# Strassen products in both feed-forward networks of a two-layer trunk, with the activations through DRAM

## The chip, the core and the metric

The kernel runs on one core of a Trainium2 chip. The metric is the device time of one execution in microseconds (us). In the text PE is the matmul engine (TensorE), PEld its weight load, DVE VectorE, ACT ScalarE, POOL GpSimd, and SP the queue that issues most DMAs.

## What is computed

Two layers over 1024 tokens of width 1024, in fp32. Layer 0 is an mLSTM (chunkwise recurrence with a gate on its output), layer 1 attention with forget gates ("fox" in the code). Behind each stands a feed-forward network (FFN), which holds the two products of this case. Norms stand before and after each block, with a residual.

```python
D_MODEL = 1024
SEQ = 1024
D_FF = 2816
CONV_WIDTH = 3
...
def conv_ffn(h, w_up, conv_w, conv_b, w_down):
    S = h.shape[1]
    u = h @ w_up
    up = jnp.pad(u, ((0, 0), (CONV_WIDTH - 1, 0), (0, 0)))
    y = conv_b
    for j in range(CONV_WIDTH):
        y = y + conv_w[j] * up[:, j:j + S]
    gate, val = jnp.split(y, 2, axis=-1)
    return (jax.nn.gelu(gate, approximate=True) * val) @ w_down
...
    # mlstm_mixer, behind the recurrence
    hs = hs.reshape(B, S, H * DV) * w_head_norm.astype(f32)
    hs = hs * jax.nn.sigmoid(o.astype(f32))
    return hs.astype(h.dtype) @ w_out
```

## The kernel before

Every fp32 operand is split in two float32r parts, hi (a cast on ACT, `split`, L155) and lo (source minus hi, on DVE, L156), and every product is three matmuls: hi by hi, hi by lo, lo by hi. The token side stands transposed in SBUF as `xh` and `xl` [128, 8, 1024]. Other SBUF space is numbered slots of [128, 1024]. PSUM is one tile of two banks, `two`, and six banks `b0` to `b5`, of 512 columns.

The FFN (`ffn`) goes through 22 column tiles f of 128. For each, gate and value are 2 x 2 x 24 matmuls of 128x512 (L689, two halves of tokens, 8 row tiles, 3 terms). The convolution reads PSUM (ACT L698, two taps on DVE L702), then gelu (L748) and the product with the value (L749); the result is split and kept in SBUF. Every two column tiles `down` adds their products for each of the 8 token tiles (L722, 1056 matmuls per layer) to accumulators `yacc` in SBUF (DVE L728). Weights are loaded one tile ahead (`load_w`, `load_rows`). The last four column tiles are added token tile by token tile; each is finished by `tail_a` (norm, residual, store) and, in the first FFN, `tail_b` (the next norm); `tail_a` multiplies on DVE (L172) and divides the residual add between POOL (L174, 416 columns) and DVE (L175). Residuals are loaded to three slots in turn, L765.

The recurrence goes through 8 chunks of 128 tokens. The output gate of all chunks is projected in four groups of 256 columns (`o_tile`, L345 tanh), stored to DRAM (`m_so`) and loaded again per chunk (`gate`). Groups 0 and 1 come before the recurrence, 2 and 3 partly among chunk 0 and 1. The output projection of chunk i-1 (`project`, L266) fills PE while DVE and ACT do chunk i. At the end 84 matmuls of the FFN's first column tile stand between the projection of chunk 7 and the transposes of its tokens (`turn_next`, by `tail_c`, L164). The attention's output projection has the same arrangement. Two helpers appear in the rows only: L242 (`acc`) is the matmuls of the mLSTM's and attention's projections and of the last token tile, and L1084 and L786 are products of two SBUF tiles on POOL, of 1024 columns in the attention and of 512 in the last tail.

The order on PE is that of the code (within `in_order`); the other engines' order is set by a scheduler from the program. The stages in the trace: projections of the mLSTM to 266.8 us, recurrence to 503.6, first FFN to about 1256, attention to about 1957, second FFN to the end.

Of the kernel before, what the change touches and what calls it, by code (L numbers as in the profile page):

```python
# [35 lines left out]
# the slots of more than 1024 columns  # L36
WIDE = {14: 1032, 31: 1032, 0: 1088, 1: 1088, 2: 1088, 3: 1088, 15: 1088, 27: 1088, 29: 1088, 30: 1088}


class Core:  # L40
    """Shared state: constants, the transposed activations in two float32r parts, the SBUF slots that every
    phase lays out for itself ([128, 1024] each), and the PSUM as one tile of two banks and six of one."""

    def __init__(self, ctx, tc):
# [14 lines left out]
        self.xh = c.tile([P, ND, S], F32R, name="xh")  # L59
        self.xl = c.tile([P, ND, S], F32R, name="xl")  # L60
# [4 lines left out]
        self.nring = 0  # L65
        self.slots = {}
# [15 lines left out]

    def wide(self, *banks):
# [12 lines left out]
    def in_order(self):  # L96
        """Within this the tensor engine takes its instructions in the order given here."""
# [31 lines left out]
    def rms_scale(self, src, root=True):  # L129
        """1 / sqrt(mean(src^2) + eps) over the free axis of a [128, 1024] view; root: from the table's root."""  # L130
# [22 lines left out]
    def split(self, hi, lo, src):  # L153
        """src in two float32r parts."""
# [3 lines left out]
    def transpose_split(self, h, hi, lo, banks):  # L158
        """h [128 rows, 8*128] -> its 8 transposed blocks, split, in hi / lo [128, 8, 128]."""
        for b in range(2):  # L160
            tp = self.b[banks[b]].rearrange("p (d t) -> p d t", d=4)
            for d in range(4):
                e = 4 * b + d
                self.nc.tensor.transpose(tp[:, d], h[:, e * P:(e + 1) * P], self.ident)  # L164
            self.split(hi[:, 4 * b:4 * b + 4], lo[:, 4 * b:4 * b + 4], tp)
# [12 lines left out]
    def tail_b(self, h, z, g, root=True):  # L178
        """h = z / rms(z), times g."""
# [1172 lines left out]
```

## Time and profile before

| | us |
|---|---|
| median of 3 runs (2700.39 to 2707.19) | 2703.64 |
| span of the profiled execution | 2699.6 |
| PE busy | 2632.5 (98%) |
| DVE busy | 1379.2 (51%) |
| ACT busy | 920.5 (34%) |
| POOL busy | 289.1 (11%) |
| weight loads (PEld) busy | 2192.3 (81%) |
| mean granted clock of PE | 0.992 |

The busy times are sums over the whole span; a stage is read from the windows of the section on rows. The profiled span leaves out what lies around the first and the last instruction.

### The profile page before, as it was taken

Reading aid. Unit: us, or ns where it says so; the run is one execution under the profiler, and the core shown is the slowest. Engines: PE = TensorE matmul, PEld = TensorE weight load, DVE = VectorE, ACT = ScalarE, POOL = GpSimd, SP = SyncE. Lnnn points to the kernel's source line nnn. Section 1 sums busy time; section 2 is a strip of 40 time slices with the busy share of each in tenths; the row PEclk is TensorE's granted clock in tenths of the full one; section 3 lists DMA queues with packets and bytes.
Section 4 is the critical chain, followed back from the end, with each engine's and each line's share of the span. In section 5 each row is a group of like instructions: output and inputs, shape, how many; then the busy total and the mean of one; then the engine's idle time right before and its main releaser. Section 6 shows DMA issues by size and latency. Waiting matters only on the chain.

```text
span 2699.6 us, 33977 instructions
## 1 busy us (share of the span) xinstructions
PE 2632.5 (98%) x13344; PEld 2192.3 (81%) x13344; DVE 1379.2 (51%) x2404; ACT 920.5 (34%) x1697; POOL 289.1 (11%) x321
## 2 busy tenths in 40 slices
PE   8999888999999999999999999999999999999998
PEld 7989877888888888888878888877888888888886
DVE  5222266644444444448565565556643455555546
ACT  5222233332222222225355455555333222222222
POOL 0001111000000000003133333322100000000001
PEclk9999899999999999999999999999999999999999
DMA  7444353311111111123755444545311111111123
GB/s 209 141 140 137 105 161 114 110 32 47 48 50 51 49 50 51 48 71 137 212 145 153 137 140 134 146 144 164 110 55 47 47 47 47 47 47 47 47 62 118
DMA packets 247133, 259.67 MB, mean 96 GB/s; under 512 B 16701, under 2 KB 208029, under 8 KB 246973
## 3 DMA queue, kind: packets, MB, share of 16 engines
q1 hardware_dynamic: 246828, 257.24, 31.9%
q8 instruction: 105, 1.72, 0.3%
q14 instruction: 56, 0.45, 0.1%
q10 hardware_dynamic: 144, 0.26, 0.0%
HBM read 193.85 MB, written 63.60 MB: 95 GB/s over the span
## 4 chain that ended last, share of the span: by engine, by line
PE 49%; DVE 3%; ACT 1%; DMA 1%; issue 1%; POOL 1%; DVEq 0%; SPq 0%; POOLq 0%; ACTq 0%
PE b L689 18%; PE b L889 9%; PE two L722 4%; PE b L722 4%; PE b L1069 2%; PE b L1057 2%; PE b L266 2%; PE two L1042 2%; PE b L906 2%; PE two L266 1%; PE b L242 1%; PE b L1042 1%; ACT junk L137 1%; DVE s L156 1%; DVE s L172 1%
## 5 line engine op out<-in xcount | busy, mean ns | idle before, releaser
L689 PE MATMUL b<-xh,s 128*128 128x512 f32 (+1 forms) x2816 | 865.5, 388 | 0.7 <-DVE xl L156 0.7
L689 PEld LDWEIGHTS b<-xh,s 128*128 128x128 f32 x2816 | 524.4, 188 | 117.8 <-DVE xl L156 0.9
L156 DVE TENSOR_TENSOR s<-s,s 128x1024 fp32r<-128x1024 f32 (+2 forms) x319 | 314.8, 997 | 496.9 <-ACT s L155 478.1
L689 PE MATMUL b<-xl,s 128*128 128x512 f32 (+1 forms) x1408 | 547.1, 389 | 0.0
L155 ACT CAST s<-s 128x1024 fp32r<-128x1024 f32 (+2 forms) x319 | 264.0, 839 | 663.0 <-PE b L722 226.2
L702 DVE SCALAR_TENSOR_TENSOR s<-b,cp,s 128x512 f32<-128x512 f32 x344 | 241.7, 745 | 232.6 <-ACT s L698 229.6
L689 PEld LDWEIGHTS b<-xl,s 128*128 128x128 f32 x1408 | 264.4, 188 | 58.3
L889 PE MATMUL b<-xh,s 128*128 128x512 f32 x768 | 274.6, 413 | 1.7 <-DVE s L156 1.1
L722 PE MATMUL two<-s,s 128*128 128x512 f32 x1056 | 258.1, 394 | 0.0
L722 PE MATMUL b<-s,s 128*128 128x512 f32 x1032 | 252.3, 394 | 0.0
L722 PEld LDWEIGHTS two<-s,s 128*128 128x128 f32 x1056 | 198.0, 188 | 46.7 <-DVE s L728 0.7
L722 PEld LDWEIGHTS b<-s,s 128*128 128x128 f32 x1032 | 193.6, 188 | 45.0
L698 ACT ACTIVATE s<-b,cp 128x512 f32<-128x512 f32 x172 | 133.1, 774 | 279.3 <-PE b L689 279.3
L242 PE MATMUL b<-s,xh 128*128 128x256 f32 (+1 forms) x864 | 163.2, 290 | 10.5 <-ACT s L345 6.7
L889 PEld LDWEIGHTS b<-xh,s 128*128 128x128 f32 x768 | 143.8, 191 | 25.4 <-DVE s L156 1.6
L889 PE MATMUL b<-xl,s 128*128 128x512 f32 x384 | 159.4, 415 | 0.0
L156 DVE TENSOR_TENSOR s<-b,s 128x512 fp32r<-128x512 f32 (+3 forms) x208 | 111.4, 564 | 75.6 <-ACT s L155 70.0
L242 PEld LDWEIGHTS b<-s,xh 128*128 128x128 f32 x864 | 137.8, 195 | 12.2 <-ACT s L345 6.9
L174 POOL TENSOR_TENSOR s<-s,s 128x416 f32<-128x416 f32 x31 | 45.9, 1480 | 886.9 <-DVE ring L144 698.7
L1049 POOL TENSOR_SCALAR s<-s,ring 128x256 f32<-128x256 f32 (+7 forms) x128 | 100.6, 789 | 313.5 <-DVE ring L1048 290.6
L242 PE MATMUL b<-s,xl 128*128 128x256 f32 (+1 forms) x432 | 124.9, 289 | 0.6 <-DVE xl L156 0.6
L155 ACT CAST s<-b 128x512 fp32r<-128x512 f32 (+3 forms) x208 | 95.9, 489 | 75.2 <-PE b L1057 61.5
(221 smaller groups left out, 3360.9 us busy)
## 6 DMA issues: line engine op xcount, KB each, us to landing
s<-in_ffn_w_up_dram SPq DMA_DIRECT2D x88, 512.0 KB, 3.8
s<-in_ffn_w_down_dram SPq DMA_DIRECT2D x44, 512.0 KB, 3.6
s<-in_mlstm_w_in_dram SPq DMA_DIRECT2D x24, 512.0 KB, 6.1
x<-s SPq DMA_DIRECT2D x24, 512.0 KB, 2.6
s<-x SPq DMA_DIRECT2D x24, 512.0 KB, 3.8
s<-in_x_dram SPq DMA_DIRECT2D x16, 512.0 KB, 4.6
s<-in_kv_w_dram SPq DMA_DIRECT2D x16, 512.0 KB, 5.0
f_v<-s SPq DMA_DIRECT2D x32, 256.0 KB, 2.6
```

The lines of the kernel that those rows point to most:

```text
L155: self.nc.scalar.copy(hi, src)
L156: self.nc.vector.tensor_tensor(lo, src, hi, ALU.subtract)
L242: self.nc.tensor.matmul(out, st, mv, start=i == 0, stop=i == n - 1)
L266: self.nc.tensor.matmul(self.at(ps, c), st, mv[:, c:c + 512], start=kk == 0 and st is sh and mv is wh, stop=kk == 7 and st is sl)
L689: nc.tensor.matmul(k.at(u, c, n), st[d], mv[:, d, cs], start=d == 0 and i == 0 and c % 512 == 0, stop=d == ND - 1 and i == 2 and c + n in ...
L698: nc.scalar.activation(y[:, a:b], v, AF.Identity, bias=cp[:, 3, col:col + 1], scale=cp[:, 2, col:col + 1])
L702: nc.vector.scalar_tensor_tensor(y[:, a + j:e], v[:, :e - a - j], cp[:, 2 - j, col:col + 1], y[:, a + j:e], ALU.mult, ALU.add)
L722: nc.tensor.matmul(k.at(ps, c), st[:, cs], mv[:, c:c + 512], start=n == 0 and i == 0, stop=n == len(items) - 1 and i == 2)
L889: nc.tensor.matmul(ps, st[d], mv[:, d, cs], start=d == 0 and i == 0, stop=d == ND - 1 and i == 2)
L906: nc.tensor.matmul(ps, st[:, d, cols], mv[d], start=d == 0 and i == 0, stop=d == ND - 1 and i == 2)
L1042: nc.tensor.matmul(ps[:, c:e], st[:, qs], mv[:, c:e], start=a == 0, stop=a == 1 and e < n)
L1049: nc.gpsimd.tensor_scalar(pt[:, :n], pt[:, :n], rd, 1.0, ALU.mult, ALU.mult)
```

## The change

Both FFN products use Strassen's scheme in Winograd's form: each operand is cut in 2 x 2 blocks, and 7 products of blocks take the place of 8, with sums of blocks as operands.

- Up product: per column tile f the 7 products (`PRODUCTS`) have 12 matmuls of 128x512 each (`up`). Sums on the token side are made once per layer, when a token tile of the second half is turned (`turn`: an add on DVE, six on POOL, splits). Sums of weights are four POOL adds of 512 columns per f (`prep_up`), with five splits. Products go from PSUM to SBUF by an ACT copy or a DVE add, and the convolution reads SBUF. The result is stored to DRAM (`act`), not kept.
- Down product: groups of 4, 3, 2 and 2 pairs of column tiles. The operands of a group are loaded from DRAM in quarters (`load_down`), summed on POOL (`sums_down`) and split (`prep_down`); 7 products over 4 token tiles of 3 matmuls for each pair (`down`).
- Output gate: groups 1 to 3 are projected for the next chunk among the parts of the recurrence (`o_more`) and stay in SBUF. The output projection no longer stands in the recurrence: `out_stage` does it behind, for the mLSTM and the attention alike, token tiles in the order 0, 4, 1, 5, 2, 3, 6, 7.
- Slots are numbered anew, some as pairs of 2048 columns, and `x` is one tile of four blocks.

```diff
+PRODUCTS = ("11", "12", "S2", "S1", "S3", "S4", "22")
...
-    def project(c, i=NT, o=None, nxt=None):
...
+        for i in range(NT):
             nxt = loads(i + 1) if i < NT - 1 else None
             nd = numerators(i, cur)
+            o_more(i + 1, 1)
+            update(i, cur, (0, 1))
+            update(i, cur, (2, 3))
             heads(i, *nd)
...
+            o_more(i + 1, 2)
+            if nxt:
+                scores(i + 1, nxt)
...
+            o_more(i + 1, 3)
...
+            turn_heads(i)
...
+        t21 = k.transposed(h, 0, banks[0])
+        nc.scalar.copy(a21, t21)
+        t22 = k.transposed(h, 1, banks[1])
+        nc.vector.tensor_tensor(s1, t22, a21, ALU.add)
...
+        for name, out, terms in (("S2", s2, ((s1, a11[0], ALU.subtract), (s2, a11[1], ALU.subtract))),
+                                 ("S3", a21, ((a11[0], a21, ALU.subtract), (a21, a11[1], ALU.add))),
+                                 ("S4", s4, ((a12[0], s2, ALU.subtract), (s4, a12[1], ALU.add)))):
+            for a, b, op in terms:
+                nc.gpsimd.tensor_tensor(out, a, b, op)
+            k.split(self.place(name, 0, m), self.place(name, 1, m), out)
...
+        elif name == "S2":
+            nc.gpsimd.tensor_tensor(t1, b12, b11, ALU.subtract)
+            nc.gpsimd.tensor_tensor(t2, b22, t1, ALU.subtract)
+            nc.gpsimd.tensor_tensor(b12, b22, b12, ALU.subtract)
+            nc.gpsimd.tensor_tensor(b21, b21, t2, ALU.subtract)
+        elif name == "S1":
+            split("T2", tmp, 1024)
...
+        for d in range(4):
+            for i, (a, b) in enumerate(((0, 0), (0, 1), (1, 0))):
+                mv = x[b](d)
+                out = bank if name in ("11", "12", "22", "S3") else bank.rearrange("p (m t) -> p m t", m=2)
+                nc.tensor.matmul(out, w[a][:, d], mv, start=first and d == 0 and i == 0, stop=d == 3 and i == 2,
+                                 skip_group_check=True)
...
+        if adds:
+            nc.vector.tensor_tensor(out, out, bank, ALU.add)
+        else:
+            nc.scalar.copy(out, bank)
...
+    GROUPS = (0, 4), (4, 3), (7, 2)
+    LAST = 9, 2
...
+        if i == 0:
+            tt("S1", "A21", "A22", add)
+            tt("A21", "A11", "A21", sub)
+            tt("A11", "S1", "A11", sub)
+            tt("B11", "B12", "B11", sub)
+            tt("T2", "B22", "B11", sub)
+            tt("B12", "B22", "B12", sub)
+        elif i == 1:
+            tt("A12", "A12", "A11", sub)
+            tt("B21", "B21", "T2", sub)
...
+        for p in range(n):
+            for e, (st, mv) in enumerate(((ah, bh), (ah, bl), (al, bh))):
+                nc.tensor.matmul(bank, st[:, p, cs], mv[:, p], start=first and p == 0 and e == 0, stop=p == n - 1 and e == 2,
+                                 skip_group_check=True)
...
+            self.load_down(0, ("A11", "B11"))
+            for name in PRODUCTS:
+                self.steps_up(f, (name,))
+                self.load_down(0, {"S2": ("A12", "B21", "A21"), "S1": ("A22", "B12"), "22": ("B22",)}.get(name, ()))
...
+    def res(self, t):
+        r = self.k.f((31, 32)[t // 4])
...
+def out_stage(k, w, gather, src, dst, gpost, gnext, f, begun=0):
...
+        y = y_of(n)
+        k.out_proj(y, t, w, begun if n == 0 else 0, 5)
+        if n > 1:
+            f.turn(z_of(n), ORDER[n - 2], (0, 1))
+        k.out_proj(y, t, w, 5, 8)
...
+    f.turn(z_of(6), ORDER[6], (0, 1))
+    f.start()
+    f.lead()
+    f.lead2()
+    f.turn(z_of(7), ORDER[7], (0, 1))
+    f.run()
```

Three places in the order of the engines, names of buffers with their numbers.

PE at the entry of the first FFN, before: the projection of chunk 7 (L266, banks b4 and b5) with the transposes of chunk 6's tokens (L164) within it.

```order
L266 MATMUL b_89<-s_130,xl 128x512
L266 MATMUL b_90<-s_130,xl 128x512
L164 MATMUL b_85<-ident,s_2933 128x128 x4
L164 MATMUL b_86<-ident,s_2933 128x128 x4
L266 MATMUL b_89<-s_131,xh 128x512
```

The same place after: end of the projection (L296), the transposes of tile 6 (s_2064), four products of column tiles 0 and 1 (L768), the transposes of tile 7 (s_129), and the third product of column tile 0.

```order
L296 MATMUL two<-p_867,x 128x512 x2
L197 MATMUL b_84<-ident,s_2064 128x128 x4
L197 MATMUL b_85<-ident,s_2064 128x128 x4
L768 MATMUL b_86<-x,s_3424 128x512 x12
L768 MATMUL b_87<-x,s_3425 128x512 x12
L768 MATMUL b_88<-x,s_3424 128x512 x12
L768 MATMUL b_89<-x,s_3425 128x512 x12
L197 MATMUL b_84<-ident,s_129 128x128 x4
L197 MATMUL b_85<-ident,s_129 128x128 x4
L768 MATMUL b_86<-p_3790,s_1828 128x512
```

Between the last two turns there were 84 matmuls of the FFN and the rest of chunk 7's projection; now there are 48 matmuls.

POOL at that place, before: the recurrence's last work, then residual adds (L174) and, much later, weights of the attention (L217).

```order
L510 TENSOR_TENSOR s_156<-s_156,decb 128x516
L174 TENSOR_TENSOR s_818<-s_818,s_2933 128x416
L174 TENSOR_TENSOR s_3121<-s_3121,s_2933 128x416
L174 TENSOR_TENSOR s_818<-s_818,s_2933 128x416
L174 TENSOR_TENSOR s_3121<-s_3121,s_2933 128x416
L217 TENSOR_TENSOR s_129<-s_129,gains 128x1088
```

After: token sums of tile 6 (L700), the residual add of tile 7 (L207), the weight sums of two column tiles (L743 to L746), and then the token sums of tile 7.

```order
L700 TENSOR_TENSOR s_3390<-x,s_3390 128x512
L207 TENSOR_TENSOR s_3420<-s_3420,s_129 128x416
L700 TENSOR_TENSOR s_3390<-s_3390,x 128x512
L743 TENSOR_TENSOR s_554<-s_4198,s_4197 128x512
L744 TENSOR_TENSOR s_554<-s_4197,s_554 128x512
L745 TENSOR_TENSOR s_4198<-s_4197,s_4198 128x512
L746 TENSOR_TENSOR s_4198<-s_4198,s_554 128x512
L743 TENSOR_TENSOR s_554<-s_4218,s_4217 128x512
L744 TENSOR_TENSOR s_554<-s_4217,s_554 128x512
L745 TENSOR_TENSOR s_4218<-s_4217,s_4218 128x512
L746 TENSOR_TENSOR s_4218<-s_4218,s_554 128x512
L700 TENSOR_TENSOR s_3390<-s_156,x 128x512
```

POOL had no sums here; now eight weight sums stand between the two tiles' token sums.

SP at the end, before: residual loads (L765) and stores of the result (L176), three slots in turn.

```order
L765 DMA s_2937<-x_93 128x1024
L765 DMA s_13654<-x_93 128x1024
L765 DMA s_13578<-x_93 128x1024
L176 DMA out_dram<-s_2937 128x1024
L765 DMA s_2937<-x_93 128x1024
L176 DMA out_dram<-s_13654 128x1024
```

After: two slots, the loads (L976) behind the stores (L209) of the pair before.

```order
L976 DMA s_156<-x_92 128x1024
L976 DMA s_2064<-x_92 128x1024
L209 DMA out_dram<-s_156 128x1024
L209 DMA out_dram<-s_2064 128x1024
L976 DMA s_156<-x_92 128x1024
L976 DMA s_2064<-x_92 128x1024
```

A load waits for a store of the round before, where one of three slots had been free.

## Rows read from the trace of the kernel before

**Rows 1.** Page, span and busy us of each engine (share of span).

```profile
span 2699.6 us, 33977 instructions
PE 2632.5 (98%) x13344; PEld 2192.3 (81%) x13344; DVE 1379.2 (51%) x2404; ACT 920.5 (34%) x1697; POOL 289.1 (11%) x321
```

**Rows 2.** Windows: stretch, length, busy by engine, granted clock, DMA share, GB/s.

```profile
0.00:12.00 12.00, 1.97 (x9) 1.60 (x9) 4.73 (x13) 5.20 (x7) 2.70 (x21) 1.00 0.86 285
...
266.80:503.60 236.80, 209.71 (x1210) 178.49 (x1208) 129.86 (x458) 76.02 (x250) 27.17 (x33) 0.94 0.44 132
503.60:1256.00 752.40, 751.79 (x3309) 610.42 (x3310) 375.05 (x488) 208.77 (x259) 20.79 (x13) 1.00 0.18 55
```

**Rows 3.** Timeline of PE after waits: start, us, instruction, idle before.

```profile
284.00 0.79 PE L242 MATMUL b<-s,xh 128*128 128x256 f32 x2 [6.73 <-ACT s L345]
...
501.30 0.66 PE L164 MATMUL b<-ident,s 128*128 128x128 f32 x4 [0.79 <-DVE s L562]
...
1266.60 0.49 PE L242 MATMUL b<-s,xh 128*128 128x272 f32 x2 [2.41 <-DVE F L852]
...
1269.56 0.66 PE L242 MATMUL b<-s,xh 128*128 128x272 f32 x2
...
1270.24 0.63 PE L242 MATMUL b<-s,xh 128*128 128x272 f32 x2
...
1270.84 0.42 PE L242 MATMUL b<-s,xh 128*128 128x272 f32 x2
```

**Rows 4.** Windows of steady FFN, PE and PEld: first L689 alone, then L722 twice.

```profile
600.00:1200.00 600.00, 417.43 (x1795) 337.04 (x1796) 1.00 0.17 51
...
600.00:1200.00 600.00, 185.32 (x796) 149.02 (x794) 1.00 0.17 51
2030.00:2600.00 570.00, 196.91 (x846) 158.40 (x844) 1.00 0.17 49
```

**Rows 5.** Timeline of PE, matmuls of 256 columns.

```profile
1965.42 0.40 PE L689 MATMUL b<-xh,s 128*128 128x256 f32 x2
...
1965.77 0.40 PE L689 MATMUL b<-xh,s 128*128 128x256 f32 x2
```

**Rows 6.** Groups by line and form: count, busy us, mean ns, idle before.

```profile
L156 DVE TENSOR_TENSOR s<-s,s 128x1024 fp32r<-128x1024 f32 x211 | 257.6, 1229 | 473.4 <-ACT s L155 461.9 <-DMA s<-m_wi 11.0 <-PE b L1069 0.5
L728 DVE TENSOR_TENSOR s<-s,b 128x512 f32<-128x512 f32 x142 | 91.1, 682 | 42.3 <-PE b L722 42.3
L749 DVE TENSOR_TENSOR s<-s,s 128x1024 f32<-128x1024 f32 x44 | 53.8, 1223 | 2.1 <-ACT s L748 1.2
L155 ACT CAST s<-s 128x1024 fp32r<-128x1024 f32 x211 | 219.1, 1048 | 622.6 <-PE b L722 226.2 <-DMA s<-in_ffn_w_up_dram 170.6 <-DVE s L749 97.2
L748 ACT ACTIVATE s<-s 128x1024 f32<-128x1024 f32 x44 | 46.6, 1060 | 137.2 <-DVE s L702 137.2
L155 ACT CAST xh<-b 128x512 fp32r<-128x512 f32 x80 | 43.5, 586 | 49.9 <-PE b L164 49.6
```

**Rows 7.** Instructions of three lines: count, min/median/max ns, first and last start.

```profile
L172 DVE SCALAR_TENSOR_TENSOR s<-s,ring,s x15: 1274/1285/2369, 1221.5 to 2689.2; 128x1024 f32<-128x1024 f32 x15
L174 POOL TENSOR_TENSOR s<-s,s x31: 1071/1633/1946, 362.0 to 2691.7; 128x416 f32<-128x416 f32 x31
L1084 POOL TENSOR_TENSOR s<-s,s x7: 2382/2393/2398, 1438.9 to 1829.6; 128x1024 f32<-128x1024 f32 x7
```

**Rows 8.** Timeline near the end, all engines: start, us, instruction.

```profile
2684.18 5.74 PE L242 MATMUL b<-s,s 128*128 128x512 f32 x24
2689.17 2.37 DVE L172 SCALAR_TENSOR_TENSOR s<-s,ring,s 128x1024 f32<-128x1024 f32 x1
2689.17 1.28 POOL L786 TENSOR_TENSOR s<-s,s 128x512 f32<-128x512 f32 x1 [2.39 <-DVE ring L146]
```

**Rows 9.** DMA issues: count, KB each, median us from issue to landing.

```profile
x<-s SPq DMA_DIRECT2D x24, 512.0 KB, 2.6
s<-x SPq DMA_DIRECT2D x24, 512.0 KB, 3.8
```

More of the change, by code (lines that the diff above doesn't have):

```diff
@@ L1 @@
 from contextlib import ExitStack
+from copy import copy
 from functools import partial
@@ L81, in r, with both, xb, xs @@
         return self.slot(i, F32R)[:, :n]
+    def both(self, j):
+        self.slot(PAIRS[j][0], F32R)
+        return self.slots[j][0]
+    def xb(self, part, h, kk):
+        o = 4096 * BLOCK[h, kk] + 2048 * part
+        return self.x[:, o:o + 2048].rearrange("p (d t) -> p d t", d=4)
+    def xs(self, part, d, c, n):
+        return self.xb(part, c // 512, d // 4)[:, d % 4, c % 512:c % 512 + n]
     def wide(self, *banks):
@@ L156, in split, with transposed @@
         self.nc.vector.tensor_tensor(lo, src, hi, ALU.subtract)
[L158 to L165, printed above, removed]
+    def transposed(self, h, b, bank):
+        tp = self.b[bank].rearrange("p (d t) -> p d t", d=4)
+        for d in range(4):
+            e = 4 * b + d
+            self.nc.tensor.transpose(tp[:, d], h[:, e * P:(e + 1) * P], self.ident)
+        return tp
     def tail_a(self, z, y, res, t, gpost, store, root=True):
@@ L186, in tail_c @@
     def tail_c(self, h, t, banks):
-        cols = slice(t * P, (t + 1) * P)
-        self.transpose_split(h, self.xh[:, :, cols], self.xl[:, :, cols], banks)
+        c = t % 4 * P
+        for b in range(2):
+            tp = self.transposed(h, b, banks[b])
+            self.split(self.xb(0, t // 4, b)[:, :, c:c + P], self.xb(1, t // 4, b)[:, :, c:c + P], tp)
     def bcast_row(self, tile_, row):
@@ L629, in mlstm @@
[L629 to L644 removed]
+        o_more(0, 2, 3)
+        for i in range(NT):
             nxt = loads(i + 1) if i < NT - 1 else None
@@ L760, in ffn @@
[L760 to L783 removed]
+            nc.vector.scalar_tensor_tensor(y[:, j:], u[:, :S - j], cp[:, 2 - j, col:col + 1], y[:, j:], ALU.mult, ALU.add)
@@ new lines, in operands @@
+    def operands(self, g, i):
+        n = self.size(g)[1]
+        if g < len(self.GROUPS):
+            s = (7 * g + i) % 2
+            v = [self.k.x[:, 8192 * s + 2048 * j:8192 * s + 2048 * j + n * 512] for j in range(4)]
+        elif i < 4:
+            s, h = ((0, 1), (1, 1), (1, 0), (0, 0))[i]
+            v = [self.k.x[:, 8192 * s + 2048 * j + 1024 * h:8192 * s + 2048 * j + 1024 * h + 1024] for j in range(4)]
+        else:
+            v = [self.k.r(j) for j in self.OPS[i - 4]]
+        v = [a.rearrange("p (g c) -> p g c", g=n) for a in v]
+        return v[:2], v[2:]
@@ new lines, in sums_down, with tt @@
+    def sums_down(self, g, i):
+        def tt(out, a, b, op):
+            for o, u, v in zip(*(self.quarter(g, name) for name in (out, a, b))):
+                self.nc.gpsimd.tensor_tensor(o, u, v, op)
+        sub, add = ALU.subtract, ALU.add
+        if i == 0:
[8 more added lines that the diff above has]
+            tt("B21", "B21", "T2", sub)
@@ new lines, with prep_down, y @@
+    HELD = ("A11", "B11"), ("A12", "B21"), ("A11", "T2"), ("S1", "B11"), ("A21", "B12"), ("A12", "B22"), ("A22", "B21")
+    def prep_down(self, g, i):
+        for name, (hi, lo) in zip(self.HELD[i], self.operands(g, i)):
+            for e, part in enumerate(self.quarter(g, name)):
+                a, b = 2 * e, 2 * e + part.shape[1]
+                self.k.split(hi[:, a:b], lo[:, a:b], part)
+        if i < 2:
+            self.sums_down(g, i)
+    def y(self, t):
+        return self.k.f((8, 9, 10, 11, 2, 6, 12, 13)[t])
@@ new lines, in down @@
+    def down(self, g, i, m, bank):
+        k, nc = self.k, self.nc
+        (ah, al), (bh, bl) = self.operands(g, i)
+        n = self.size(g)[1]
+        first = i in (0, 1, 3)
+        cs = slice(m * P, (m + 1) * P)
+        for p in range(n):
+            for e, (st, mv) in enumerate(((ah, bh), (ah, bl), (al, bh))):
+                nc.tensor.matmul(bank, st[:, p, cs], mv[:, p], start=first and p == 0 and e == 0, stop=p == n - 1 and e == 2,
+                                 skip_group_check=True)
+        t, c = ((m, 0), (m, 0), (m, 512), (m + 4, 512), (m + 4, 512), (m, 512), (m + 4, 0))[i]
+        y = self.y(t)[:, c:c + 512]
+        if (t, c) in self.seen:
+            nc.vector.tensor_tensor(y, y, bank, ALU.add)
+        else:
+            nc.scalar.copy(y, bank)
+            self.seen.add((t, c))
@@ new lines, in res, with tail, final @@
+    def res(self, t):
+        r = self.k.f((31, 32)[t // 4])
+        self.nc.sync.dma_start(r, self.src[t * P:(t + 1) * P, :])
+        return r
+    def tail(self, t, gpb):
+        k, y = self.k, self.y(t)
+        res = self.res(t)
+        k.tail_a(y, y, res, t, gpb, self.dst)
+        if self.follow is not None:
+            k.tail_b(y, res, None)
+    def final(self, t, gpb):
+        k, nc, y = self.k, self.nc, self.y(t)
+        cs = slice(t * P, (t + 1) * P)
+        res = self.res(t)
+        parts = [(y[:, a:b], a, b) for a, b in ((512, D), (0, 512))]
@@ L974, in fox @@
     yield
-    for t in range(NT):
+    for t in ORDER:
         v_tile(0, t, w0, (4, 5))
```

574 lines of the change are left out of this document (279 added, 295 removed), and 3 rows, old and new, of the table AT.

## The prediction

> **What bounds the kernel now.** I read the page's busy times first: TensorE works 2632.5 of 2699.6 us, VectorE about half of the span, ScalarE a third, GpSimd a tenth [rows 1]. Hence what is taken from TensorE shortens the run one for one, as long as the other engines deliver in time; what is given to VectorE, ScalarE or GpSimd is free until one of them is late. The share is an average, so next I read the windows by stage [rows 2]. The first FFN (503.6 to 1256) is pure TensorE, 751.79 of 752.40 us at full clock; VectorE has 375 us of work there, ScalarE 209, GpSimd 21, and DMA is at 0.18. The recurrence with its output projection (266.8 to 503.6) is looser: TensorE 209.7 of 236.8 us, clock 0.94, VectorE 130. Its waits are of the kind in [rows 3]: 6.73 us behind the last output-gate tanh, and after each longer wait the granted clock is at the lower of its two levels for a while. At 1269.56 a pair of 272-column matmuls takes 0.66 us, at 1270.84 it takes 0.42, and three of them with their neighbour start 0.68 us apart (1269.56 to 1270.24), where 816 columns at 0.2327 us for 512 would be 0.37. From 1266.6 to 1270.2 the work runs at about half speed, so a restart costs some 1.7 us beyond the wait.
>
> The price of a matmul comes from dividing within steady FFN stretches [rows 4]: L722 took 185.32 us for 796 and 196.91 us for 846, 0.2328 us per 128x512 matmul. L689 gives 417.43/1795 = 0.2326. I use 0.2327.
>
> **Matmuls removed: -184.3 us.** Before, a layer's up product is 22 column tiles x 2 (gate, value) x 2 token halves x 8 x 3 = 2112 matmuls, the down product 22 x 8 x 2 x 3 = 1056. After, each column tile has 7 half-size products of 12 matmuls (1848), the down product 7 x 4 token tiles x 3 x 11 pairs (924). Over two layers 6336 become 5544; 792 x 0.2327 = 184.3 us. Every one had been on the path [rows 2]. The products S1, S2 and S4 read 512 columns as two runs of 256. No row shows that form; the nearest are 256-column matmuls, three in 0.35 us (1965.42 to 1965.77) [rows 5], two of them 0.234 us. For 792 such matmuls I take +2 us, range 0 to 5.
>
> **The up product in steady state: hidden.** A column tile costs TensorE 84 x 0.2327 = 19.55 us. Beside it VectorE has two adds and three low parts of 512 columns (0.68 each), two low parts of 1024 (1.23), four taps of the convolution of 1024 (1.285, as L172) and the product of gate and value (1.22): 3.4 + 2.5 + 5.1 + 1.2 = 12.2 us [rows 6, 7]. ScalarE has three casts and four copies of 512 (0.59), two casts of 1024 (1.05), two convolution starts and a gelu (1.06): about 10 us [rows 6]. GpSimd has four adds of 512 at 1.28 [rows 8]: 5.1 us. So all fit, if they run beside each other. Do VectorE and GpSimd? At 2689.17 both start: GpSimd's add takes its usual 1.28 us, VectorE's L172 takes 2.37 instead of 1.285 [rows 7, 8], longer by 1.09, nearly the other's time. The Trainium skill says why (SBUF — State Buffer, "Who interferes with whom"): a VectorE instruction with two SBUF inputs and a GpSimd instruction that reads SBUF share a port pair as an exclusive lock, and the loser blocks fully. It speaks against this change, which multiplies GpSimd's two-input adds, and the row agrees; by the page nothing but the exclusion is added, so it too gives the 17.3 us worked out next. Taking the row at full weight, the two engines exclude each other: 12.2 + 5.1 = 17.3 us, still under 19.55. I therefore take 0 here; the margin is 2.2 us, and its loss is a rival below. The output goes to DRAM (loads of 3.8 us, stores of 2.6 us [rows 9]) with DMA nearly idle: hidden.
>
> **FFN entry: +45 us (24 to 60).** The third product of the first column tile (S2) needs the token sums of tile 7, the last that the output projection makes. Before it TensorE has, after turning tile 6, only four lead products, 48 x 0.2327 = 11.2 us, and two turns of tile 7: busy for about 12.1 us. What tile 7 needs is queued behind other things on each engine. On GpSimd its six sums (L700) come after five sums and an L207 add of tile 6, one more L700 and the eight weight sums L743 to L746 of two column tiles. Counting from tile 6's turn, tile 6's VectorE add ends at 1.5, five GpSimd adds at 1.28 end at 7.9, L207 (about 1.4) at 9.3, the next add at 10.6, eight weight sums at 20.8. ScalarE holds the square of tile 7's second norm behind the cast of that sixth sum (10.6), and the root behind the cast of weight sums; with VectorE's low parts ahead of L217 the normed tile comes at 20 to 23. TensorE's fourth lead product also waits for weights whose low part stands behind L217, to 23 to 26. Then two turns, VectorE's S1 (28), two GpSimd adds (31) and a split: S2 can start at 29 to 32 us. Minus 12.1 that is 17 to 20 us of waiting, plus two restarts, about 4 us [rows 3]: 22.5 per layer. If the scheduler's weight sums run early, 12; if GpSimd's adds lengthen as L174 did, from 1.07 to a median of 1.63 [rows 7], 30. Twice: +45. Before, this place has gaps below 1 us (0.79 at 501.30 [rows 3]).
>
> **Entry of the down product: +29 us (16 to 44).** Group 0 (four pairs) loads 8 MB from DRAM; at the 285 GB/s of the start [rows 2] that is 29 us, begun in the last column tile, so the last operands land 1 to 10 us after the last up product. Then GpSimd runs eleven 1024-column sums up to the one that product 2 needs, 11 x 2.39 (L1084) [rows 7] = 26.3 us. Ready at 29 to 36, plus 2 for the split. TensorE has only products 0 and 1, 2 x 48 x 0.2327 = 22.4 us: a wait of 9 to 16, plus restart, 14.5 per layer (8 to 22). Later groups prepare under the products of the group before, of 78, 59 and 39 us: nothing.
>
> **Last group: +15 us (4 to 25).** With two residual slots for three, the four tail rounds of the end run store 2.6, load 3.8 [rows 9] and add 1.6 in a row, 8.0 us a round. VectorE has 50 to 56 us of adds and tails there for 39 us of TensorE. After TensorE begins the group, the second layer ends at about 60 us, against 39 + 9.7 if only the present end remained (last matmul ends 2689.9, span 2699.6 [rows 1, 8]): +11. In the first layer +4.
>
> **mLSTM: -11 us (-25 to +3).** Gate tiles go between the parts of the recurrence and remove the DRAM round trip; the matmuls stay. From 216 to 503.7, 254.9 us of TensorE work (its matmul columns in the code at 0.2327 us for 512) stand in 287.7 us, 32.8 us of waits and low clock (27.1 of it idle in 266.8 to 503.6 [rows 2]). After, each chunk has 17.2 us of TensorE work, of which 11 cover a VectorE chain of some 8, so most waits go; at the end, the output projection no longer fills the chain of chunk 7, and the casts of its weights stand ahead in the queues: 12 us and restarts, 20 to 22 left in all. **Fox output: +3 (0 to 8)**, one residual slot and weights asked for later.
>
> **Sum.** 2699.6 - 184.3 + 2 + 45 + 29 + 15 - 11 + 3 = 2598.3 us of span. The median of the runs, 2703.6, is 4.0 above the profiled span, so 2602 us.
>
> **Rivals.** *A, transitions hidden*: the sums of GpSimd get done before TensorE wants them, at both FFN entries and down entries. 2602 - 45 - 29 = 2528 us. For it: GpSimd is idle nine tenths of the time now; against: the queue order puts weight sums ahead of the last token tile, and the down sums need operands which exist only at the end. *B, slower*: the exclusion of [rows 8] works in full and the column tile becomes bound by VectorE and GpSimd. GpSimd's 5.1 us lengthened as L174's worst against its best (1.946/1.071 = 1.82) are 9.3; with 12.2 that is 21.5 us, 2.0 above TensorE's, + 86 us over 44 tiles, 2688. It turns slower from a cycle of 22.04 us (2.49 x 44 = 110 us), so with another 0.6 us of semaphore and queue waits per tile: 2715 us. Against it: the sum counts the same collision twice. The page named above states this exclusion as a rule. *C, evacuations late*: each product's bank is wanted again 2.8 us later; a VectorE add of 0.69 behind a blocked tap of 2.37 is late by some tenths, twice a tile: about 1 us x 44 = + 44, 2646 us. *The change not doing what it says* would be 7 products costing as 8: bounded above by the two-run operands, +5.
>
> **Chances.** Forecast 0.76, A 0.10, C 0.10, B 0.04. The range 2550 to 2650 covers the terms' bounds combined (all at their low ends give 2538, at their high ends 2664) and half of C; it leaves out A and B. A difference of 0.3% (8 us) is what a measurement of this kernel tells from none. Faster 0.95: forecast, A, and C nearly whole; within 0.3% 0.015, slower 0.035, both from B and the edge of C.
>
> **What would show it.** TensorE busy falls by about 184 us, and its idle time is in a few places: one gap of 10 us or more at the third product of each FFN (releaser a low part or GpSimd sum), one at the third product of down group 0, and an end after the last matmul of 15 to 25 us. Within an FFN no gap in a column tile, a cycle near 19.6 us. Wrong if the cycle is above 20 us (C or B), if the entries have no gap (A), or if the matmuls of S1, S2 and S4 take longer than 0.24 us each.

## Result and profile after

The changed kernel takes 2789.1 us (median; 2787.6 to 2793.6), the kernel before 2704.1: ratio 1.0313, interval 1.0298 to 1.0328. It is 3.1% slower, where 3.8% faster was forecast. The profiled span is 2791.7 us, 193 us above the forecast 2598.

The first lines of its page (span; busy us, share and count by engine) answer to [rows 1].

```profile
span 2791.7 us, 33870 instructions
PE 2507.9 (90%) x12456; PEld 2074.6 (74%) x12456; DVE 1683.6 (60%) x2520; ACT 1163.0 (42%) x2072; POOL 890.1 (32%) x641
```

PE has 124.6 us less work (not 184, since more of it runs at a lower clock: 0.954 in the mean, 0.992 before), but 90% of a longer span is 284 us of idle time, where 67 us had been. The windows by stage answer to [rows 2]: length, busy us of PE, PEld, DVE, ACT, POOL, clock, DMA share, GB/s.

```profile
287.00:449.00 162.00, 118.10 (x792) 104.15 (x790) 63.63 (x238) 44.55 (x177) 18.84 (x28) 0.86 0.29 76
...
557.00:625.00 68.00, 44.67 (x160) 34.55 (x160) 46.20 (x50) 27.79 (x44) 37.52 (x25) 0.77 0.19 57
625.00:1031.00 406.00, 405.22 (x1758) 330.37 (x1759) 263.84 (x269) 200.21 (x252) 126.22 (x80) 1.00 0.29 94
...
1130.00:1250.00 120.00, 92.04 (x363) 73.28 (x363) 91.98 (x96) 39.07 (x44) 62.97 (x24) 0.90 0.21 71
```

In this order they are the recurrence, the entry of the first FFN, its up product in steady state (with the first matmuls of the down product), and the middle of its down product. Only the third is as full as the FFN before. What PE waited for (engine and its line, releaser, total us, times, longest) names the losses:

```profile
PE two L904 <- DVE s L909: 115.2, 37, 20.5
PE b L549 <- DVE s L556: 43.0, 6, 9.0
PE b L768 <- DVE s L190: 26.7, 4, 9.2
PE b L768 <- ACT p L189: 12.1, 2, 6.2
```

L904 is the down product's matmul and L909 the add of its result, L549 the recurrence's state update and L556 the add of it, L768 the up product. Stage by stage, cut at the last matmul of the output projections and of the down products (in the kernel before without the FFN's twelve lead matmuls):

| stage | before | after | change | forecast |
|---|---|---|---|---|
| to the end of the first output projection | 515.8 | 556.4 | +40.6 | -11 |
| first FFN | 739.3 | 755.1 | +15.8 | -50 |
| attention | 702.0 | 714.1 | +12.1 | +3 |
| second FFN and end | 742.5 | 766.1 | +23.6 | -43 |

The forecasts of the FFNs are 92.2 us of matmuls less, 1 us for the split runs, and the waits of the prediction (22.5 + 14.5 + 4 and + 11). Within the first FFN the up product, entry included, takes 462.5 us and the down product 292.6, where their matmuls alone are 430.0 and 215.0 at 0.2327 us. In the second they take 461.2 and 294.4.

### The profile page after: what moved, and what is told of

Same layout as the page of the kernel before. It is cut to its first block, busy times and chain, and to the rows that moved or that the text cites. A ratio compares the mean times of both kernels' runs of the same rounds, so it can differ in the third digit from the quotient of the medians.

```text
span 2791.7 us, 33870 instructions
## 1 busy us (share of the span) xinstructions
PE 2507.9 (90%) x12456; PEld 2074.6 (74%) x12456; DVE 1683.6 (60%) x2520; ACT 1163.0 (42%) x2072; POOL 890.1 (32%) x641
## 4 chain that ended last, share of the span: by engine, by line
PE 69%; DVE 11%; issue 6%; DMA 5%; POOL 5%; ACT 4%; SPq 1%; DVEq 0%; POOLq 0%; ACTq 0%
PE b L768 30%; PE b L1107 9%; PE b L904 5%; PE b L277 5%; PE two L904 4%; PE two L277 3%; DVE x L190 3%; DMA s<-m_R 3%; PE b L1286 2%; DVE s L909 2%; PE b L1274 2%; PE two L1259 2%; POOL s L700 2%; PE b L1123 1%; POOL s L867 1%
## 5 line engine op out<-in xcount | busy, mean ns | idle before, releaser
L768 PE MATMUL b<-x,s 128*128 128x512 f32 x2112 | 510.3, 398 | 26.7 <-DVE s L190 26.7
L768 PEld LDWEIGHTS b<-x,s 128*128 128x128 f32 x2112 | 403.1, 191 | 118.9 <-DVE s L190 28.5
L189 ACT CAST s<-s 128x512 fp32r<-128x512 f32 (+3 forms) x350 | 242.6, 698 | 435.9 <-PE b L768 356.5
L190 DVE TENSOR_TENSOR s<-s,s 128x512 fp32r<-128x512 f32 (+3 forms) x344 | 283.7, 830 | 228.6 <-ACT s L189 221.1
L768 PE MATMUL b<-p,s 128*128 128x512 f32 x1584 | 388.0, 398 | 14.9 <-ACT p L189 12.1
L768 PEld LDWEIGHTS b<-p,s 128*128 128x128 f32 x1584 | 301.2, 190 | 87.2 <-ACT p L189 12.6
L1107 PE MATMUL b<-x,s 128*128 128x512 f32 x1104 | 333.1, 413 | 0.0
L904 PE MATMUL b<-x 128*128 128x512 f32 x1248 | 294.8, 395 | 9.4 <-DVE x L190 5.6
L904 PEld LDWEIGHTS b<-x 128*128 128x128 f32 x1248 | 238.6, 192 | 63.0 <-DVE x L190 7.4
L785 DVE SCALAR_TENSOR_TENSOR s<-s,cp,s 128x1023 f32<-128x1023 f32 (+1 forms) x176 | 242.1, 1376 | 29.7 <-ACT s L783 28.0
L904 PE MATMUL two<-x 128*128 128x512 f32 x456 | 132.7, 440 | 108.8 <-DVE s L909 107.5
L1107 PEld LDWEIGHTS b<-x,s 128*128 128x128 f32 x1104 | 200.5, 190 | 31.1
L746 POOL TENSOR_TENSOR s<-s,s 128x512 f32<-128x512 f32 x44 | 94.1, 2138 | 360.6 <-DMA s<-in_ffn_w_up_dram 330.7
L904 PEld LDWEIGHTS two<-x 128*128 128x128 f32 x456 | 93.9, 212 | 141.0 <-DVE s L909 119.3
L190 DVE TENSOR_TENSOR x<-s,x 128x1024 fp32r<-128x1024 f32 (+2 forms) x110 | 168.7, 1556 | 40.2 <-ACT x L189 39.1
L277 PE MATMUL b<-s,x 128*128 128x256 f32 (+1 forms) x824 | 126.0, 298 | 12.1 <-DVE x L190 6.8
L207 POOL TENSOR_TENSOR s<-s,s 128x416 f32<-128x416 f32 x31 | 45.0, 1452 | 247.8 <-DVE s L205 214.5
```

Of the source, the lines that this page charges most:

```text
L189: self.nc.scalar.copy(hi, src)
L190: self.nc.vector.tensor_tensor(lo, src, hi, ALU.subtract)
L277: self.nc.tensor.matmul(out, st, mv, start=i == 0, stop=i == n - 1)
L746: nc.gpsimd.tensor_tensor(b21, b21, t2, ALU.subtract)
L768: nc.tensor.matmul(out, w[a][:, d], mv, start=first and d == 0 and i == 0, stop=d == 3 and i == 2, skip_group_check=True)
L785: nc.vector.scalar_tensor_tensor(y[:, j:], u[:, :S - j], cp[:, 2 - j, col:col + 1], y[:, j:], ALU.mult, ALU.add)
```

## Experiments

Each kernel is the changed kernel with one edit; times are spans of one profiled execution unless a ratio is given. Spans of stages that an edit doesn't touch differ between these kernels by up to 5 us: the first output projection ends between 551.3 and 556.4 where nothing there was edited (556.4 is the changed kernel itself), and an up product with its entry takes 459.5 to 462.7. So a stage is compared with itself and small differences are not read.

### The recurrence: m_exps

The timeline after, one chunk (start, us, engine, line, operation, idle before and its releaser):

```profile
304.28 1.58 SPq L518 DMA_DIRECT2D s<-m_R  x1
...
316.06 1.09 POOL L524 TENSOR_SCALAR_AFFINE_SELECT s<-s 128x1024 f32<-128x1024 f32 x1 [9.74 <-DMA s<-m_R]
317.18 0.40 ACT L528 ACTIVATE s<-s,gcols 128x128 f32<-128x128 f32 x1 [8.86 <-POOL s L524]
317.49 0.26 ACT L579 ACTIVATE junk<-b 128x128 bf16<-128x128 f32 x1
...
321.15 0.17 DVE L585 SCALAR_TENSOR_TENSOR ring<-ring 128x8 f32<-128x8 f32 x1 [8.92 <-ACT junk L579]
...
322.70 0.28 DVE L556 TENSOR_TENSOR s<-s,b 64x129 f32<-64x129 f32 x1
...
323.43 2.14 PE L549 MATMUL b<-s,p 128*128 128x258 f32 x4 [8.40 <-DVE s L556]
```

Read it from below. PE's second pair of state updates wants banks that DVE's adds L556 empty. These stand behind L585, which wants ACT's squares L579 of the current chunk. On ACT the squares stand behind and between the exponentials L528 of the next chunk, which want POOL's mask L524, which wants a load of about 11 us. The load serves the next chunk, which is needed only later: nothing but the place in ACT's queue puts it into the chain. The edit writes mask and exponentials behind the chunk's heads and keeps ACT to that order.

```diff
-    with k.in_order():
+    with k.tc.manual_schedule(engines={mybir.EngineType.PE, mybir.EngineType.Activation}):
...
             o_more(i + 1, 2)
             if nxt:
+                exps(i + 1, nxt)
                 scores(i + 1, nxt)
```

> The changed kernel with the exponentials of the next chunk's decay matrix written behind the current chunk's heads and ScalarE kept to the order of the program within the recurrence. Theory 3 (ScalarE holds the squares of the current chunk behind exponentials that wait for a DMA of 11 us, and VectorE's state updates wait for the squares, which TensorE waits for 8.4 us per chunk): the five gaps of 7.5 to 9 us at the state update go below 3 us, TensorE's clock there rises, and the recurrence gets 35 to 55 us shorter, total 2737 to 2757. Rival (the chain through VectorE itself, numerators to state, takes these 8 us): the gaps stay above 6 us, gain below 12 us.

Measured: span 2750.0, the first output projection ends at 516.8 for 556.4, 39.6 us earlier (34.5 against the earliest kernel with this stage unedited). Theory 3 holds; the edit moves mask, exponentials and ACT's order together, so their shares are not told apart. In its timeline the squares (L582 here) start at once, and the wait at the update (L552) is short:

```profile
293.43 0.28 ACT L582 ACTIVATE junk<-b 128x128 bf16<-128x128 f32 x1 [0.51 <-DVE ring L579]
...
298.68 0.70 PE L552 MATMUL b<-s,p 128*128 128x258 f32 x2 [1.74 <-DVE s L559]
```

### The down product: d_memset, d_vector, d_banks, d_both

In the down product DVE's low parts (L190, and the last taps L785) and POOL's sums (L867) run in turn. A piece of the timeline after:

```profile
1026.76 3.38 POOL L867 TENSOR_TENSOR p<-p,p 128x1024 f32<-128x1024 f32 x1
1027.81 3.41 DVE L785 SCALAR_TENSOR_TENSOR s<-s,cp,s 128x1022 f32<-128x1022 f32 x1
1030.10 3.39 POOL L867 TENSOR_TENSOR s<-p,s 128x1024 f32<-128x1024 f32 x1
1031.14 3.43 DVE L190 TENSOR_TENSOR x<-s,x 128x1024 fp32r<-128x1024 f32 x1
```

A sum takes 2.39 us alone, a low part 1.23 and a tap 1.28 [rows 6, 7]; side by side each shows 3.4, so the two together get one of each done in 3.3 us (the sums start 3.3 us apart). That is nearly the 3.6 us of doing them one after the other.

```diff
 # d_memset
-                self.nc.gpsimd.tensor_tensor(o, u, v, op)
+                self.nc.gpsimd.memset(o, 0.0)
+                self.nc.gpsimd.memset(o, 0.0)
+                self.nc.gpsimd.memset(o[:, :, :256], 0.0)
 # d_vector
-                self.nc.gpsimd.tensor_tensor(o, u, v, op)
+                self.nc.vector.tensor_tensor(o, u, v, op)
 # d_banks
-        a, b = k.b[:4], k.b[4:] + two
+        a, b = k.b[:4], [k.b[4], two[0], k.b[5], two[1]]
...
```

> The changed kernel with each GpSimd sum of down operands replaced by GpSimd memsets of the same tile for about the same time (2.25 tiles' worth of writes), so GpSimd is as long busy at the same places but reads nothing; the block sums are left out. Theory 2 (GpSimd's two-input reads and VectorE's two-input low parts exclude each other, 1.23 us parts take 3.3): low parts return to 1.23 us, the sums no longer stretch to 3.3, and the down products get 20 to 35 us shorter per layer, total 2720 to 2750. Rival (only the order of the queues matters, the waiting for late sums): the stretch of the down products stays within 8 us of 293 us each, total above 2775.

Measured: 2687.1; the down products take 243.8 and 244.2 us, 48.9 and 50.2 less, more than theory 2 asked for. Not all of it need be exclusion: a memset reads no operand, so the memsets begin 14 us before the end of the last up product, where the sums begin 2 us behind it. What d_memset shows by itself is the length of the low parts. Here are groups of DVE in the first down product (count, busy us, mean ns, idle before), first after, then d_memset with one of POOL's memset groups:

```profile
L190 DVE TENSOR_TENSOR x<-s,x 128x1024 fp32r<-128x1024 f32 x24 | 51.1, 2131 | 17.0 <-ACT x L189 16.9
```

```profile
L190 DVE TENSOR_TENSOR x<-s,x 128x1024 fp32r<-128x1024 f32 x28 | 34.0, 1220 | 16.9 <-ACT x L189 16.9
L868 POOL MEMSET s<- 128x1024 f32 x17 | 16.1, 957 | 0.3
```

Beside POOL's writes a low part lasts 1.22 us, for 2.13 beside its sums, and the memsets keep to 0.96: writes alone stretch neither engine. The Trainium skill says this too (SBUF — State Buffer, "Who interferes with whom": a VectorE instruction with two SBUF inputs contends with GpSimd's reads, not with one that only writes), and the runs agree.

> The changed kernel with the sums of down operands on VectorE instead of GpSimd. If the exclusion is the cost (theory 2): eleven sums of 1.23 us instead of 2.39, nothing stretched, group 0 starts some 13 us earlier, and the down products get 15 to 30 us shorter per layer, total 2730 to 2760. Rival (VectorE's load is the bound): 0.5 us a token step more VectorE work makes the groups of 2 and 3 pairs longer, total 2790 to 2830.

Measured: 2732.1; the down products take 265.0 and 265.7, 27.6 and 28.7 us less. Theory 2 holds against the rival that DVE is full: it takes over the sums at 1.22 us each and is no longer busy than before (222.1 us in both, by windows over the first down product), because what it loses to sums it gains from low parts of 1.22 us. The 28 us are the price of having the sums on POOL: the exclusion, and that a sum alone takes 2.39 us there and 1.22 on DVE. No run separates the two.

> One edit to the changed kernel: in the down products the two halves of the two-bank PSUM tile no longer take adjacent token tiles (they alternate with b4, b5), and in the last group no product uses both halves. Theory 1 (a half of that tile cannot be written while the other half's sum is being read, so each such pair exposes VectorE's queue to TensorE): the 0.78 us gaps vanish and the 5 to 7.6 us gaps of groups 0 to 2 shrink; 25 to 45 us per layer, total 2700 to 2740. Rival (VectorE, slowed by GpSimd's sums, is simply the bound of the down products, and the waits come back on other banks): under 10 us per layer, total above 2770.

Measured: 2757.0; the down products take 272.7 and 279.8, 19.9 and 14.6 us less, under the 25 to 45 of theory 1 and over the 10 of its rival. In the first layer 5.3 us of it come back in the attention stage (719.4 us for 714.1), so some 15 us a layer are left. Theory 1 is half right. Here is what the edit removes, after (PE and DVE around 1188):

```profile
1185.46 2.20 PE L904 MATMUL two<-x 128*128 128x512 f32 x9
...
1188.04 2.77 DVE L190 TENSOR_TENSOR x<-s,x 128x1024 fp32r<-128x1024 f32 x1
...
1191.33 2.76 DVE L190 TENSOR_TENSOR x<-s,x 128x1024 fp32r<-128x1024 f32 x1
...
1194.01 0.68 DVE L909 TENSOR_TENSOR s<-s,two 128x512 f32<-128x512 f32 x1
1194.74 4.21 PE L904 MATMUL two<-x 128*128 128x512 f32 x9 [7.08 <-DVE s L909]
```

PE has filled one half of `two` and does not write the other until DVE has read the first (whether the program or the chip asks for this was not tested); DVE's add of 0.68 us stands behind low parts of 2.8. Where DVE is free, the same pair costs 0.78 us or a little more, some 15 times a layer. With other tiles between the halves these short gaps are gone, but waits of 3.8 to 10.2 us remain in the middle groups, and the 18.4 us of group 0: DVE's queue, stretched by POOL, is late for any bank.

> The changed kernel with the edits of d_banks and d_vector only. If the two costs are separate: down products of about 245 us per layer as in c_three, span 2695 to 2702, and the remaining 40 us to c_three are the recurrence's. If m_exps had helped the down products: above 2710.

Measured: 2701.6, down products 244.3 and 247.4 us, 48.3 and 47.0 less; the single edits sum to 47.5 and 43.3. The costs add up, so they are separate within some 4 us. These two edits alone bring the kernel to the time of the one before: one run of 2703.4 us against a median of 2703.4.

### The up product's margin: u_double

```diff
             nc.gpsimd.tensor_tensor(t1, b12, b11, ALU.subtract)
             nc.gpsimd.tensor_tensor(t2, b22, t1, ALU.subtract)
+            nc.gpsimd.tensor_tensor(t1, b12, b11, ALU.subtract)
+            nc.gpsimd.tensor_tensor(t2, b22, t1, ALU.subtract)
+            nc.gpsimd.tensor_tensor(t1, b12, b11, ALU.subtract)
+            nc.gpsimd.tensor_tensor(t2, b22, t1, ALU.subtract)
```

> The changed kernel with two of the four weight sums of each column tile done three times (eight GpSimd sums for four, the same values). It measures the margin of the up product. If VectorE and GpSimd excluded each other in full, 12.2 + 10.2 = 22.4 us a column tile would exceed TensorE's 19.55 and the two layers would take up to 125 us more (span above 2860). If only the parts that meet exclude each other, as the 2.37 us of the one row did, the column tile stays near 19.6 us and the span within 15 us of 2791.7 plus the longer entries (10 us per layer): 2792 to 2825.

Measured: 2885.4, 93.7 us more. The span is above the 2860 that was set for full exclusion; a column tile takes 21.3 us for 19.4, nearer to 22.4 than to 19.6, and the clock stays at 1.00. PE's timeline in it shows the same wait in two column tiles, and the second fence DVE and POOL ahead of the second wait:

```profile
819.51 3.03 PE L772 MATMUL b<-p,s 128*128 128x512 f32 x12 [1.66 <-DVE s L778]
...
840.81 0.50 PE L772 MATMUL b<-p,s 128*128 128x512 f32 x1 [1.66 <-DVE s L778]
```

```profile
833.80 2.31 DVE L190 TENSOR_TENSOR s<-s,s 128x1024 fp32r<-128x1024 f32 x1
...
834.99 2.29 POOL L749 TENSOR_TENSOR s<-s,s 128x512 f32<-128x512 f32 x1
...
836.03 2.33 DVE L789 SCALAR_TENSOR_TENSOR s<-s,cp,s 128x1023 f32<-128x1023 f32 x1
...
840.08 0.68 DVE L778 TENSOR_TENSOR s<-s,b 128x512 f32<-128x512 f32 x1
```

The wait is for the evacuation L778, which stands behind stretched low parts and taps. So rival C's mechanism and B's exclusion exist, at the place that the prediction gave; with four sums a tile the margin holds, with eight it is gone. The changed kernel shows why it holds (groups from 625 to 1031):

```profile
L190 DVE TENSOR_TENSOR s<-s,s 128x1024 fp32r<-128x1024 f32 x39 | 47.7, 1223 | 68.7 <-ACT s L189 68.7
L746 POOL TENSOR_TENSOR s<-s,s 128x512 f32<-128x512 f32 x19 | 42.4, 2234 | 178.7 <-DMA s<-in_ffn_w_up_dram 169.3 <-issue 9.5
```

Three of the four sums stay near 1.29 us (1.29 to 1.35 in the mean), since they run where DVE reads PSUM or is idle. Only the fourth, L746, meets two-input work of DVE, and there POOL pays: DVE's low parts stay at 1.22 us in the mean.

### The entry of an FFN: e_lead, e_weights

The timeline after at the entry of the first FFN:

```profile
578.39 4.56 PE L768 MATMUL b<-x,s 128*128 128x512 f32 x12 [9.01 <-DVE s L190]
...
583.51 1.89 DVE L217 SCALAR_TENSOR_TENSOR s<-s,ring,s 128x1024 f32<-128x1024 f32 x1
...
587.12 4.64 PE L768 MATMUL b<-x,s 128*128 128x512 f32 x10 [4.17 <-DVE s L190]
...
591.55 1.24 PE L197 MATMUL b<-ident,s 128*128 128x128 f32 x8
...
598.78 0.79 PE L768 MATMUL b<-p,s 128*128 128x512 f32 x1 [5.99 <-ACT p L189]
```

Tile 7 is normed by 585.4, but its transposes L197 come at 591.6, behind the lead products of column tile 1, whose weights' low parts are late.

```diff
 # e_lead
     f.lead()
-    f.lead2()
     f.turn(z_of(7), ORDER[7], (0, 1))
+    f.lead2()
 # e_weights
+            eng = nc.vector if f < 2 else nc.gpsimd
-            nc.gpsimd.tensor_tensor(t1, b12, b11, ALU.subtract)
+            eng.tensor_tensor(t1, b12, b11, ALU.subtract)
...
```

> The changed kernel with the two lead products of the second column tile behind the turn of token tile 7 instead of ahead of it. Theory 4 (at the entry of an FFN tile 7 is turned late since TensorE's order puts a product ahead of it whose weights' low part is itself late): the turn comes at about 587 instead of 591.5, the two products cover the sums, 4 to 9 us less per layer, span 2774 to 2784. Rival (the sums on GpSimd behind eight weight sums alone set the third product): below 2 us per layer.

Measured: 2769.6; the up products with their entries take 455.1 and 452.9 us, 7.4 and 8.3 less. Theory 4 holds in size; the rest of the span's 22 us lies in stages that the edit doesn't touch. One wait is left, for L217, the norm of tile 7 itself:

```profile
581.46 1.94 PE L197 MATMUL b<-ident,s 128*128 128x128 f32 x8 [17.07 <-DVE s L217]
```

PE's idle time in the first up product falls by only 2.1 us (24.7 to 22.6); the other 5 are shorter busy time (437.8 to 432.5), with a granted clock of 0.82 over the 68 us of the entry (552 to 620) where three waits left 0.77.

> The changed kernel with the weight sums of the first two column tiles of each FFN on VectorE (0.68 us each) instead of GpSimd (1.28). Theory 5 (the weight sums ahead of tile 7's token sums, and the low parts that they stretch, make the wait at the entry): 5 to 12 us less per layer, span 2768 to 2782. Rival (the chain from the last projection over the norm to the turn sets it): below 3 us per layer, or a loss, since VectorE's queue gets 5 us longer there.

Measured: 2773.4; the up products take 457.1 and 456.8, 5.4 and 4.4 less, and 2.4 and 2.9 below the lowest of the kernels with this stage unedited. That is the low edge of theory 5 at most: the weight sums ahead of tile 7's are a small part, and the wait at the third product, which they were to explain, is still 5.8 us in the first layer. That the norm's chain is the larger part is argued from the 17.1 us of e_lead; no run shortens it.

### All together: c_three, c_best

> The three edits of d_banks, d_vector and m_exps together. Alone they gave 33, 58 and 40 us (2791.7 to 2757.0, 2732.1 and 2750.0 of span). If theories 1 to 3 name separate costs they add up except where banks and sums meet in the down products: span 2665 to 2690, below the kernel before. Rival (VectorE is the bound of the down products once its sums are there): banks give nothing more, 2690 to 2700.

Measured: 2657.9, 133.8 us less and below the expected 2665; the single edits sum to 34.7 + 59.6 + 41.7 = 136.0, so they add up. Its edit of the recurrence keeps ScalarE's order to the end of chunk 7; c_best does so to chunk 5, and has the edit of e_lead.

> c_three with the edit of e_lead, and ScalarE kept to the program's order only in chunks 0 to 5 of the recurrence (in c_three TensorE waits 12.95 us at 388.6 in chunk 6, where the casts of the output weights stand ahead). Theories 3 and 4: e_lead's 7 to 8 us per layer carry over, and the wait of 13 us shrinks to that of the changed kernel there (below 3): span 2628 to 2645, ratio to before 0.972 to 0.979. Rival (the waits at the end of the recurrence and at the FFN entry only move to the next wait): 2650 to 2660, ratio 0.980 to 0.984.

Measured: median 2643.5 us, ratio 0.978 to the kernel before, interval 0.9767 to 0.9794; span 2636.5. It beats both kernels. The wait of 12.95 us is down to 0.61, but one of 6.49 us stands at a state update of chunk 6, so the first output projection ends 7.1 us earlier (506.6 for 513.7), less than was expected; the up products with their entries gain 5.8 and 8.4 (455.0 and 452.6 for 460.8 and 461.0). What it still waits for most:

```profile
PE b L197 <- DVE s L217: 34.5, 3, 17.0
PE b L915 <- DVE x L190: 21.9, 2, 11.2
PE two L915 <- DVE s L920: 20.6, 15, 2.7
```

That is the norm of tile 7 at both entries, the second operand of down group 0, and the evacuations of the later groups. By the stages of the table above, c_best differs from the kernel before by -9.2, -39.7, +18.9 and -33.0 us, where -11, -50, +3 and -43 were forecast: with ACT's order, the lead product, the sums and the banks set right, three of the four stages come within 2 to 10 us of the forecast, and the attention becomes the worst.

## Why the prediction was wrong

**Matmuls and the steady up product: right.** From 625 to 1031, 1758 matmuls take 405.2 us, 0.2305 us each, and PE is full. The products with two runs of 256 columns (S1, S2, S4) cost no more: the page's mean is 398 ns for them and for the others, whose records overlap, so that term was 0. The cover of 19.4 us held; u_double shows that it would not hold much more.

**"Later groups prepare under the products of the group before: nothing".** This is the largest failed step. I had made the sum of exclusive times for the up product and not for the down product. The first down product takes 77.6 us above its matmuls, where 18.5 were forecast (14.5 + 4), the second 79.4. Of the 77.6, 64.0 are idle time (21.9 at the entry, 28.8 between 1086 and 1236, 13.3 in the last group), and the rest is work at a lower clock (0.90 from 1130 to 1250). For the 28.8 nothing had been forecast. Two causes are shown: sums on POOL, which exclude DVE's low parts (d_memset, d_vector: 28 us a layer by moving the sums), and adjacent halves of one PSUM tile, which expose each delay of DVE's queue (d_banks: some 15 us).

**Entry of the down product, 14.5 us: mis-sized by the same cause, and the wait was put at the wrong place.** The forecast was one gap at the third product, for its sums. The gaps are 3.0 us, after 56 matmuls, and 18.9 us, after 84, when the last token tile of the second product is due:

```profile
1034.63 5.53 PE L904 MATMUL b<-x 128*128 128x512 f32 x16 [3.00 <-DVE x L190]
...
1051.13 8.84 DVE L190 TENSOR_TENSOR x<-s,x 128x1024 fp32r<-128x1024 f32 x3 [3.31 <-ACT x L189]
...
1059.89 1.27 DVE L909 TENSOR_TENSOR s<-s,b 128x512 f32<-128x512 f32 x2
...
1061.82 4.63 PE L904 MATMUL two<-x 128*128 128x512 f32 x10 [18.91 <-DVE s L909]
```

PE waits for DVE's adds, which stand behind the low parts of late sums. So the late sums are the root, as forecast, but they reach PE a product earlier, through DVE's queue. Eleven sums at 2.39 were 26.3 us; in the trace they run from 1021.05 to 1055.6, 34.5 us, since beside the low parts and taps a sum lasts up to 3.4. With sums on DVE (d_vector) the gaps are 11.1 and 2.2 us.

**mLSTM, -11 us: the sign was wrong.** "Each chunk has 17.2 us of TensorE work, of which 11 cover a VectorE chain of some 8, so most waits go" left out ACT's queue, through which a load of 11 us enters the chain. ACT's queue held the same load in the trace of before (L491 the exponentials, L543 the squares, L184 the norm's product, L520 the update's add):

```profile
389.33 0.69 ACT L491 ACTIVATE s<-s,gcols 128x128 f32<-128x128 f32 x2 [9.62 <-POOL s L487]
...
391.73 0.26 ACT L543 ACTIVATE junk<-b 128x128 bf16<-128x128 f32 x1
...
393.36 1.29 DVE L184 SCALAR_TENSOR_TENSOR s<-s,ring,s 128x1024 f32<-128x1024 f32 x1
...
394.68 1.20 DVE L520 TENSOR_TENSOR s<-s,b 64x129 f32<-64x129 f32 x4
...
395.32 1.27 PE L164 MATMUL b<-ident,s 128*128 128x128 f32 x8 [3.00 <-DVE s L520]
```

There too the squares come behind exponentials that waited 9.6 us for the mask. The adds L520 stand behind another norm's product there, not behind the squares, and PE, which wants the banks that they empty, waits only 3.0 us, with the output projection (L266) running from 384 to 392. That moving the projection out took this cover away is read from the traces; no run tests it alone. m_exps gives 35 to 40 us back, and ends near the time of before (516.8 against 515.8), not 11 us below: the end of the recurrence still waits (12.95 and 6.5 us in c_three). The wait of 13 us came with the edit's order for ACT (0.85 us there in the changed kernel). With that order kept to chunk 5 alone (c_best) the projection ends at 506.6, 9.2 us below before, so the forecast gain was there; what the step had wrong is ACT's order.

**FFN entry, 22.5 us per layer: the waits were right, the rest 9 to 10 low.** 462.5 - 430.0 = 32.5 us and 461.2 - 430.0 = 31.2, just above the forecast's range of 12 to 30. The waiting was forecast as 17 to 20 us and is 19.2 in the first layer, but in three pieces (9.0, 4.2 and 6.0), of which only the last is at the third product. Too small were the two restarts, set at 4 us: the granted clock is 0.77 from 557 to 625, and PE's busy time, with the two turns, is 7.8 us above the 430.0. A wait of 4.1 us ahead of tile 6's turn was not in the sum. The order on PE, a lead product ahead of tile 7's turn, is 7 to 8 us of the whole (e_lead), the weight sums at most 4 to 5 (e_weights).

**Last group and end, +15 us: mis-sized.** From the group's first matmul the second layer ends after 70.3 us, where 60 were forecast; the end after the last matmul is 10.5 us against 9.7 before. In the first layer the group's gaps are about 13 us against 4 forecast. Most of them are of the two halves of `two`, which were not in the sum: d_banks removes all but 1.7 us in the first layer, and with it the second ends after 61.3 us. The residual slots were not tried. **Attention, +3: it became +12.** Waits of 1 to 3 us at its first projections (1312 to 1352) are part of it; no run was made on this.

**Rivals.** A is out, since all four entries wait, and C's late evacuations show in the up product only in u_double. B forecast the right sign from the exclusion, at the wrong place: it put it into the column tile, where PE's 19.4 us cover it, and not into the groups of the down product. Its chance of 0.04 came from treating the up product as the only place where the two engines meet.

## What to carry to other kernels

Where VectorE and GpSimd both read two SBUF tiles, add their times to begin with (here 3.3 us for 3.6), in every stage and not only in the busiest; GpSimd's idle share says nothing on what a sum there costs. Before work is moved out of a loop, list what waits it covers, engine queue by engine queue, since a load far from the path can stand in the path through the order of a queue. Saved matmuls are worth their time only where the engine that feeds and empties the banks keeps its slack: here 184 us of them were lost to 217 us more of idle time and some 60 us of work at a lower clock.

## What the runs showed of the hardware

Both engines can pay at once: in a steady alternation a sum of 2.39 us and a low part of 1.23 both last 3.3 to 3.4 us, while adds with one operand in PSUM stay at 0.68 (L909) beside the same sums, and memsets of 0.95 us neither stretch nor are stretched. A tap of 1.28 us or a low part of 1.23 beside a 512-column sum of 1.28 shows up to 2.3 us (u_double's L789 by mean 1.91 and 1.71 us for 1.33), and the sum 2.1 to 2.3. In the changed kernel's up product the sum alone is longer (L746, 2.23 us).
